# A hybrid attention block: constants merged so that matmul operands begin at multiples of 1024 bytes, and a background stream of weight sums paused in four gate blocks

## The chip, the cores and the metric

The kernel runs on one core of a Trainium2 chip. Its time is the device time of one execution in microseconds (us), as the median of several runs. A profiled execution gives the trace; its span is the time from the first to the last instruction.

## What is computed

One layer on 256 rows of 2048 features, all in float32. Heads have 128 features.

```python
h = rms_norm(x, g_mix)
proj = h @ w_in          # fq fk fv f_logit | sq sk sv | mq | 3 x 2048 gates
o_fox = forgetting attention, 6 heads, of normed fq, fk and of fv
o_sb  = stick-breaking attention, 6 heads, of sq, sk, sv
o_mem = attention of normed mq on 256 memory rows, 4 heads (rms_norm(mem) @ w_mem_kv)
g = sigmoid(gates + b_gate)
merged = g[0] * (o_fox @ w_br_fox) + g[1] * (o_sb @ w_br_sb) + g[2] * (o_mem @ w_br_mem)
x = x + merged @ w_out
h2 = rms_norm(x, g_ffn)
u = causal_depthwise_conv(h2 @ w_up)          # 2 x 5632 columns, 3 taps
u_gate, u_val = split(u)
out = x + (silu(u_gate) * u_val) @ w_down
```

## The kernel before, in words

**Split operands.** Every float32 matrix product is made of products of a 4-byte type that TensorE streams faster (`F32R`). Each weight piece is loaded as `raw` (128 partitions by 1024 elements) by a DMA that SyncE (SP) issues; ScalarE casts it to a high half `hi`, VectorE subtracts to get a low half `lo`. A product then takes three matmuls of 512 columns, activations high by weights high, low by high, high by low (lines 152 to 154, 286 to 288). In the up stage (lines 1146 to 1157) weights are the stationary operand: one matmul of 512 columns takes `hi` against both halves of the activations `hT`, one of 256 columns takes `lo` against the high half.

**Stages, in TensorE's order.** Memory keys and values; then products with `w_in` (`mq`, `f0` to `f4`, `s0` to `s4`) with the attention heads worked in between; the gates; the branch products (`b0` to `b3`); `w_out` (`o`); the up stage, 22 passes of four column tiles each (`u`, 11 groups of gate columns and 11 of value columns, each pass 16 steps of four pairs of matmuls); `w_down` (`d`). TensorE's instructions stand in program order in the gates, the branch products and most other stages.

**Blocks by seven.** Some pairs of k rows are multiplied with seven block products instead of eight (`seven`, `seven_here`, an "s" in a plan string; "e" is a pair by eight). They need sums of weight blocks (`T1` to `T4`) and of activation blocks (`FS1` to `FS4`). In the gates, `g_plans` gives four blocks with three such pairs each: `02`, `10`, `11`, `12`. Their weight sums are made on the spot: `prepared` issues two loads and four VectorE additions of 512 columns a pair.

**The stream of weight sums.** For `w_out` and `w_down` the weight sums are made ahead, in the background, by the generator `weight_sums` (lines 243 to 274). One round handles one half of a pair: two loads into a staging tile `pre`, then three VectorE additions (lines 267 to 269, of 512, 256 and 256 columns), then a store of the result to device memory (`kept`). There are 58 such halves, 14 for `w_out` and 44 for `w_down`. A later block by seven reads the `kept` sums in place of weights. The generator advances by one at each `tick()`: `period` is the number of ticks of a round, `add` the ticks between loads and additions, `store` those between loads and store, `slower` is added to the period once the attention heads are done ("heads" in `issued`). `tick` also advances the foreground generators (attention heads, transposes, gathers), and with `beside=False` only these. The first stream runs from the first projections to the end of the branch products ("merged"); what is left is made by two streams in the up stage (line 1088), with staging tiles of their own, a period of 8 and starts of 14 and 16 ticks.

**Order of the engines.** VectorE, ScalarE and SP work through their instructions in order. A scheduler places the instructions that are not pinned by `in_order`, so a changed tick changes the order on VectorE and SP around it.

**Addresses.** Tiles stand behind each other in SBUF in the order in which their pools and names come: `cst` (identity, `xres`, constants, `rbc`), then `wp` (`raw`, `hi`, `lo`), then `xt_pool` (`xT`, `hT`), `sm`, and the pools of the stage. A small tile takes a multiple of 32 bytes per partition. Before the change `qscale` is made 104 elements wide although one is used. In the program as built, `raw` begins at byte 40448 of a partition and `hi`, `lo`, `xT`, `memT`/`oT`/`aT` and the 14 blocks at 512 plus a multiple of 1024; `xres` (17920) does so too.

Of the kernel before, what the change touches and what calls it, by code (L numbers as in the profile page):

```python
# [9 lines left out]
F32 = mybir.dt.float32  # L10
# [5 lines left out]
P = 128  # L16
S = 256
NT = S // P
# [3 lines left out]
N_FOX, N_SB, N_MEM = 6, 6, 4  # L22
# [19 lines left out]
def hybrid_block(  # L42
# [28 lines left out]
    cst = ctx.enter_context(tc.tile_pool(name="cst", bufs=1))  # L71
# [9 lines left out]
    def bank(name):  # L81
        return pp.tile([P, 512], F32, tag="bank", name=name)
# [14 lines left out]
    def later(gen):  # L97
        waiting.append(gen)
# [3 lines left out]
    def tick(beside=True):  # L102
        if beside:
            for g in background:
                next(g, None)
        while waiting and len(active) < WINDOW:
            active.append([waiting.popleft(), 0])
        for a in list(active):
            if a[1] > 0:
                a[1] -= 1  # L110
                continue
            try:
                a[1] = next(a[0]) or 0
            except StopIteration:
                active.remove(a)
# [208 lines left out]
    def blocked(name, w, nb, n0, plan, pair, sums, raw_tile, t4_tile, gathered, ready=None, form=None, apart=None):  # L324

        wv = by_k(w)
        X = [[bank(f"x{name}{nb}_{t}_{n}") for n in range(2)] for t in range(NT)]
        Y = []
        ns = plan.count("s")

        def a_of(p, j, t):
            v = pair(p, j)
            return v[:, t * P : (t + 1) * P], v[:, S + t * P : S + (t + 1) * P]

        def f_of(p, f):
            v = sums(p, f)
            return v[:, 0], v[:, 1]

        def load(k):
            raw = raw_tile(f"raw_{name}{nb}_{k}")  # L340
            nc.sync.dma_start(raw, wv[:, k, n0 : n0 + PIECE])
            return raw

        def eight(p, first, last):
            by_bank = last and apart is not None
            w = []
            for j in range(2):
                w.append(parts(load(2 * p + j), f"{name}{nb}_{2 * p + j}"))
                if not by_bank:
                    for t in range(NT):  # L350
                        for n in range(2):
                            three(X[t][n], *a_of(p, j, t), w[j][n], first and j == 0, last and j == 1)
                tick()
            if by_bank:
                for t in range(NT):
                    for n in range(2):
                        m = 256 if (t, n) == (1, 1) else 512
                        for j in range(2):
                            wj = [part[:, :m] for part in w[j][n]]
                            three(X[t][n][:, :m], *a_of(p, j, t), wj, last=j == 1)  # L360
                        if m < 512:
                            apart.append(bank("apart")[:, m:])
                            for j in range(2):
                                wj = [part[:, m:] for part in w[j][n]]
                                three(apart[0], *a_of(p, j, t), wj, j == 0, j == 1)

        def seven(p, first, last):
            kept = sums_of[name, nb, p]
            raw0 = raw_tile(f"raw_{name}{nb}_{2 * p}")
            nc.sync.dma_start(raw0[:, :512], wv[:, 2 * p, n0 : n0 + 512])  # L370
            nc.sync.dma_start(raw0[:, 512:], kept[:, T3])
            raw1 = load(2 * p + 1)
            raw2 = raw_tile(f"raw_t_{name}{nb}_{p}")
            nc.sync.dma_start(raw2.rearrange("p (n c) -> p n c", n=2), kept[:, 0:4:3])
            raw3 = t4_tile(f"raw_t4_{name}{nb}_{p}")
            nc.sync.dma_start(raw3, kept[:, T4])
            B00, T3w = parts(raw0, f"{name}{nb}_{2 * p}")
            three(Y[0], *a_of(p, 0, 0), B00, first, last)
            three(Y[3], *f_of(p, FS3), T3w, first, last)
            B10, B11 = parts(raw1, f"{name}{nb}_{2 * p + 1}")  # L380
            three(X[0][0], *a_of(p, 1, 0), B10)
            three(X[0][1], *f_of(p, FS4), B11)
            tick()
            T1w, T2w = parts(raw2, f"t_{name}{nb}_{p}")
            three(Y[2], *f_of(p, FS1), T1w, first, last)
            three(Y[1], *f_of(p, FS2), T2w, first, last)
            (T4w,) = parts(raw3, f"t4_{name}{nb}_{p}")
            three(X[1][0], *a_of(p, 1, 1), T4w)
            tick()

        def prepared(p):
            raw0, raw1 = load(2 * p), load(2 * p + 1)
            t13, t42 = (t4_tile(f"t{i}_{name}{nb}_{p}") for i in range(2))
            b0, b1, u, v = (w.rearrange("p (n c) -> p n c", n=2) for w in (raw0, raw1, t13, t42))
            nc.vector.tensor_tensor(u[:, 0], b0[:, 0], b0[:, 1], ALU.add)
            nc.vector.tensor_tensor(u[:, 1], b0[:, 1], b1[:, 1], ALU.add)
            nc.vector.tensor_tensor(v[:, 1], u[:, 0], b1[:, 1], ALU.add)
            nc.vector.tensor_tensor(v[:, 0], v[:, 1], b1[:, 0], ALU.add)
            return raw0, raw1, t13, t42

        def seven_here(p, first, last):
            raw0, raw1, t13, t42 = ahead.pop(p)
            (B00,) = parts(raw0[:, :512], f"{name}{nb}_{2 * p}")
            three(Y[0], *a_of(p, 0, 0), B00, first, last)
            B10, B11 = parts(raw1, f"{name}{nb}_{2 * p + 1}")
            three(X[0][0], *a_of(p, 1, 0), B10)
            three(X[0][1], *f_of(p, FS4), B11)
            tick()
            T1w, T3w = parts(t13, f"t_{name}{nb}_{2 * p}")
            three(Y[2], *f_of(p, FS1), T1w, first, last)  # L410
            three(Y[3], *f_of(p, FS3), T3w, first, last)
            T4w, T2w = parts(t42, f"t_{name}{nb}_{2 * p + 1}")
            three(X[1][0], *a_of(p, 1, 1), T4w)
            three(Y[1], *f_of(p, FS2), T2w, first, last)
            tick()

        by_seven = seven_here if name == "g" else seven
        ahead = {}
        s, e = 0, ns
        for i, c in enumerate(plan):  # L420
            if c == "s":
                if s == 0:
                    if ready:
                        ready()
                    Y += [bank(f"y{name}{nb}_{j}") for j in range(4)]
                by_seven(s, s == 0, s == ns - 1)
                s += 1
                if s == ns:
                    later(gathered(n0, Y))
            elif c == "f":  # L430
                form()
            else:
                eight(e, i == 0, i == len(plan) - 1)
                e += 1
            if name == "g" and plan[i + 1 : i + 2] == "s":
                ahead[s] = prepared(s)
        finish()
        return X
# [42 lines left out]
    nc.gpsimd.affine_select(  # L481
        after_r, ones, pattern=[[-1, P]], compare_op=ALU.is_gt, fill=0.0, base=0, channel_multiplier=1
    )
    qscale = cst.tile([P, 104], F32, name="qscale")[:, :1]
    nc.vector.memset(qscale, SCALE)

    keep_busy(7)
# [61 lines left out]
        nc.vector.tensor_reduce(tot, ss, AX.X, ALU.add)  # L549
        rsqrt_mean(dst, tot, NT, D, name)  # L550

    rpair = cst.tile([P, 2, NT], F32, name="rpair")
    rstd, rneg = rpair[:, 0], rpair[:, 1]
    rstd_m = cst.tile([P, NT], F32, name="rstd_m")
    rstd_f = cst.tile([P, NT], F32, name="rstd_f")
    ssm = cst.tile([P, NT, 4], F32, name="ssm")
    ssx = cst.tile([P, NT, 4], F32, name="ssx")
    ssf = cst.tile([P, NT, 4], F32, name="ssf")
# [4 lines left out]
    gp = mix.enter_context(tc.tile_pool(name="gp", bufs=3))  # L563
# [108 lines left out]
    for k in range(KT):  # L672
# [18 lines left out]
        for _ in range(0 if k < 3 else 1 if k < 8 else 3):  # L691
            if squares:
                j, t = squares.popleft()
# [27 lines left out]
    def weighted(pT, v, h, oh, o):  # L721
# [7 lines left out]

    ps = proj(C_MQ, MEM_W, "mq")  # L730
    background.append(
        weight_sums(lambda name: gp.tile([P, 1024], F32, tag="pre", bufs=1, name=name), 5, 4, "merged", slower=3, add=2)
    )
    finish()
    qm = heads_of(block("qm"))
# [43 lines left out]
        nc.scalar.activation(vf[0][:, t], ps[t], AF.Copy, scale=rstd[:, t : t + 1])  # L779
    ps = proj(2048, 262, "f4")  # L780
    vf[1] = rows_of(block("vf1"))
    fl = cst.tile([P, NT, N_FOX], F32, name="fl")
    for t in range(NT):
        nc.scalar.activation(vf[1][:, t, :256], ps[t][:, :256], AF.Copy, scale=rstd[:, t : t + 1])
        nc.vector.scalar_tensor_tensor(
            fl[:, t], ps[t][:, 256:262], rstd[:, t : t + 1], bfor, ALU.mult, ALU.add
        )

    lf = cst.tile([P, NT, N_FOX], F32, name="lf")
    ab = cst.tile([P, NT, N_FOX], F32, name="ab")  # L790
    cq = cst.tile([P, NT, N_FOX], F32, name="cq")
    nc.scalar.activation(ab, fl, AF.Abs)
    nc.scalar.activation(ab, ab, AF.Exp, scale=-1.0)
    nc.scalar.activation(ab, ab, AF.Ln, bias=1.0)
# [160 lines left out]
    for m in range(2):  # L955
        gate = []
        for b, plan in enumerate(g_plans[m]):
            g, bias = [], []
# [26 lines left out]
            def ready():  # L985
                finish()
                if "heads" not in issued:
                    issued.add("heads")
                    later(sigmoids(gate[0] + gate[1]))
                biases()  # L990
# [23 lines left out]
        for n in range(2):  # L1014
            acc = gate[branches[0][3]][n]
            for i, (w, k0, nk, b) in enumerate(branches):
# [5 lines left out]
                for t in range(NT):  # L1022
                    g = gate[b][n]
# [227 lines left out]
```

## Time and profile before

| What | us |
|---|---|
| median of three runs | 1480.76 (1480.16 to 1483.44) |
| the profiled execution: its time | 1481.42 |
| the profiled execution: its span | 1479.7 |
| busy in the span: TensorE matmuls | 1470.7 (99%) |
| VectorE | 1192.9 (81%) |
| ScalarE | 839.5 (57%) |
| DMA queue of SP, share of 16 engines | 78.0% |

The granted TensorE clock was full throughout. A row of a group or of the timeline names the line, the engine, the operation, the tiles as out<-in, shapes and count. PE is TensorE, PEld its weight loads, DVE VectorE, ACT ScalarE, POOL GpSimd, SPq the DMA queue of SP. A matmul's duration (0.39 us for 512 columns) is longer than the distance to the next one's start, since matmuls overlap; distances of starts are what counts for the time. In brackets stands how long the engine was idle before, and who ended it.

### The profile page before, as it was taken

The page shows a single profiled execution, that of the slowest core. Times are in us where ns is not written, and L with a number is a line of the kernel's source. Part 1 is how long each engine was busy: PE and PEld are TensorE (multiplying, and loading weights), DVE is VectorE, ACT ScalarE, POOL GpSimd, SP SyncE. Part 2 cuts the span into 40 slices and gives each one's busy share as a digit, 9 for nine tenths or more (in the row PEclk, how much of TensorE's full clock was granted, in tenths as well). Part 3 has the DMA queues.
Part 4 walks back from the last instruction along what each step waited for, and adds up shares of the span by engine and source line. Part 5 has one row for each costly group of instructions (what it writes and reads, how often), then busy time and mean ns, then how long its engine had stood idle before and what let it go on. Part 6 is the DMA issues. An engine that isn't in the chain of part 4 may idle for free.

```text
span 1479.7 us, 20666 instructions
## 1 busy us (share of the span) xinstructions
PE 1470.7 (99%) x7337; PEld 1238.4 (84%) x7337; DVE 1192.9 (81%) x1818; ACT 839.5 (57%) x1194; POOL 18.6 (1%) x46
## 2 busy tenths in 40 slices
PE   9999999999999999999999999999999999999998
PEld 7888888888888878888888888888888888888887
DVE  5777676777688899988888889888777677997877
ACT  6755454455364455545666556556556565674664
POOL 0000000011000000000000000000000000000000
PEclk9999999999999999999999999999999999999999
DMA  9687797677877687978768889888766666798896
GB/s 306 202 274 222 219 297 229 206 248 252 282 238 251 215 273 254 299 239 289 256 204 274 275 277 292 264 279 282 212 186 177 195 182 202 237 318 270 260 328 224
DMA packets 205526, 369.42 MB, mean 250 GB/s; under 512 B 13530, under 2 KB 82030, under 8 KB 205166
## 3 DMA queue, kind: packets, MB, share of 16 engines
q1 hardware_dynamic: 204094, 365.99, 78.0%
q10 hardware_dynamic: 1328, 2.11, 0.4%
q8 instruction: 57, 0.93, 0.3%
q14 instruction: 47, 0.39, 0.1%
HBM read 335.54 MB, written 32.51 MB: 249 GB/s over the span
## 4 chain that ended last, share of the span: by engine, by line
PE 90%; DVE 5%; DMA 3%; issue 1%; ACT 1%; POOL 0%; SPq 0%; DVEq 0%; ACTq 0%; POOLq 0%
PE u L1154 22%; PE u L1155 11%; PE xd L287 4%; PE xd L286 4%; PE xd L288 4%; PE f L288 2%; PE f L286 2%; PE f L287 2%; PE s L286 2%; PE s L288 2%; PE s L287 2%; PE xg L288 2%; PE g L286 2%; PE g L288 2%; PE g L287 2%; PE xg L286 2%
## 5 line engine op out<-in xcount | busy, mean ns | idle before, releaser
L1154 PE MATMUL u<-hT,hi_u 128*128 128x512 f32 x1232 | 436.2, 399 | 0.0
L1155 PE MATMUL u<-hT,lo_u 128*128 128x256 f32 x1232 | 345.9, 281 | 0.0
L142 DVE TENSOR_TENSOR lo_u<-raw_u,hi_u 128x1024 fp32r<-128x1024 f32 x176 | 215.4, 1224 | 86.4 <-ACT hi_u L141 84.8
L1154 PEld LDWEIGHTS u<-hT,hi_u 128*128 128x128 f32 x1232 | 231.5, 188 | 57.5
L141 ACT CAST hi_u<-raw_u 128x1024 fp32r<-128x1024 f32 x176 | 184.7, 1050 | 147.7 <-PE u L1154 128.9
L1155 PEld LDWEIGHTS u<-hT,lo_u 128*128 128x128 f32 x1232 | 232.7, 189 | 0.0
L281 DVE TENSOR_TENSOR lo_d<-raw_d,hi_d 128x1024 fp32r<-128x1024 f32 x88 | 106.7, 1222 | 20.5 <-ACT hi_d L280 17.8
L280 ACT CAST hi_d<-raw_d 128x1024 fp32r<-128x1024 f32 x88 | 92.0, 1054 | 48.2 <-PE xd L287 22.2
L280 ACT CAST hi_g<-raw_g 128x1024 fp32r<-128x1024 f32 (+1 forms) x64 | 61.9, 972 | 39.2 <-DMA raw_g<-in_w_in_dram 16.1
L281 DVE TENSOR_TENSOR lo_g<-raw_g,hi_g 128x1024 fp32r<-128x1024 f32 (+1 forms) x64 | 71.3, 1120 | 3.4 <-ACT hi_g L280 3.3
L141 ACT CAST hi_f<-raw_f 128x1024 fp32r<-128x1024 f32 (+1 forms) x40 | 38.6, 967 | 51.2 <-PE f L287 46.5
L286 PE MATMUL xd<-hi_d,aT 128*128 128x512 f32 x170 | 66.2, 389 | 0.0
L288 PE MATMUL xd<-lo_d,aT 128*128 128x512 f32 x170 | 66.2, 389 | 0.0
L287 PE MATMUL xd<-hi_d,aT 128*128 128x512 f32 x170 | 66.1, 389 | 0.0
L142 DVE TENSOR_TENSOR lo_f<-raw_f,hi_f 128x1024 fp32r<-128x1024 f32 (+1 forms) x40 | 44.7, 1119 | 25.7 <-ACT hi_f L141 23.1
L141 ACT CAST hi_s<-raw_s 128x1024 fp32r<-128x1024 f32 (+1 forms) x40 | 38.4, 960 | 45.0 <-PE s L287 25.5
L1154 PE MATMUL u<-hT_rest,hi_u 128*128 128x512 f32 x176 | 63.1, 398 | 0.0
L142 DVE TENSOR_TENSOR lo_s<-raw_s,hi_s 128x1024 fp32r<-128x1024 f32 (+1 forms) x40 | 44.7, 1118 | 22.7 <-ACT hi_s L141 22.1
L141 ACT CAST hi_b<-raw_b 128x1024 fp32r<-128x1024 f32 x32 | 33.7, 1052 | 50.9 <-DMA raw_b<-in_w_br_sb_dram 16.0
L1126 ACT ACTIVATE y<-u,taps 128x256 f32<-128x256 f32 x88 | 49.3, 595 | 13.2 <-DVE u L1123 13.2
L142 DVE TENSOR_TENSOR lo_g<-raw_g,hi_g 128x1024 fp32r<-128x1024 f32 x32 | 39.2, 1229 | 21.1 <-ACT hi_g L141 20.8
L288 PE MATMUL xg<-lo_g,xT 128*128 128x512 f32 x140 | 54.8, 392 | 1.2 <-DVE lo_g L281 1.2
(481 smaller groups left out, 3509.5 us busy)
## 6 DMA issues: line engine op xcount, KB each, us to landing
raw_u<-in_w_up_dram SPq DMA_DIRECT2D x176, 512.0 KB, 4.7
raw_g<-in_w_in_dram SPq DMA_DIRECT2D x96, 512.0 KB, 4.7
raw_d<-in_w_down_dram SPq DMA_DIRECT2D x66, 512.0 KB, 5.1
pre_d<-in_w_down_dram SPq DMA_DIRECT2D x88, 256.0 KB, 4.3
kept_d<-pre_d SPq DMA_DIRECT2D x44, 512.0 KB, 5.3
raw_f<-in_w_in_dram SPq DMA_DIRECT2D x32, 512.0 KB, 5.0
raw_s<-in_w_in_dram SPq DMA_DIRECT2D x32, 512.0 KB, 5.0
raw_o<-in_w_out_dram SPq DMA_DIRECT2D x25, 512.0 KB, 6.3
```

The lines of the kernel that those rows point to most:

```text
L141: pin(nc.scalar.copy(hi[:, :m], raw[:, :m]))
L142: pin(nc.vector.tensor_tensor(lo[:, :m], raw[:, :m], hi[:, :m].bitcast(F32), ALU.subtract))
L280: nc.scalar.copy(hi[:, :n], src)
L281: nc.vector.tensor_tensor(lo[:, :n], src, hi[:, :n].bitcast(F32), ALU.subtract)
L286: fix(nc.tensor.matmul(o, lhsT=ah, rhs=w[0], start=first, stop=False))
L287: fix(nc.tensor.matmul(o, lhsT=al, rhs=w[0], start=False, stop=False))
L288: fix(nc.tensor.matmul(o, lhsT=ah, rhs=w[1], start=False, stop=last))
L1126: nc.scalar.activation(y, u[:, 2:], AF.Identity, scale=tap(2), bias=tap(3))
L1154: nc.tensor.matmul(ps[i], lhsT=hi[:, j, c], rhs=hT(k + j), start=first, stop=False)
L1155: nc.tensor.matmul(ps[i][:, :S], lhsT=lo[:, j, c], rhs=hT(k + j)[:, :S], start=False, stop=last)
```

## The change

Three edits.

1. In blocks called with the name "g", that is the four gate blocks with pairs by seven, ticks advance the foreground alone: `tick()` in `eight`, `seven` and `seven_here` becomes `go_on()`, which is `tick(beside=name != "g")`. The stream stands still there and goes on in the branch products.
2. The first stream's period goes from 5 to 6 ticks, and `slower` from 3 to 2. What it has not done by "merged" is done by the two streams of the up stage, whose own numbers are unchanged.
3. `rpair`, `rstd_m` and `rstd_f` become one tile `scales`, `fl`, `lf`, `ab` and `cq` one tile `logits`, and `qscale` loses its unused columns. The tiles behind them begin 512 bytes earlier: `raw` at byte 39936, and `hi`, `lo`, `xT`, `memT`/`oT`/`aT` and the blocks at multiples of 1024. `xres` stays where it is.

```diff
+        go_on = lambda: tick(beside=name != "g")
+
         def eight(p, first, last):
...
                             three(X[t][n], *a_of(p, j, t), w[j][n], first and j == 0, last and j == 1)
-                tick()
+                go_on()
...
         def seven_here(p, first, last):
...
             three(X[0][1], *f_of(p, FS4), B11)
-            tick()
+            go_on()
...
             three(Y[1], *f_of(p, FS2), T2w, first, last)
-            tick()
+            go_on()
...
-    qscale = cst.tile([P, 104], F32, name="qscale")[:, :1]
+    qscale = cst.tile([P, 1], F32, name="qscale")
...
-    rpair = cst.tile([P, 2, NT], F32, name="rpair")
-    rstd, rneg = rpair[:, 0], rpair[:, 1]
-    rstd_m = cst.tile([P, NT], F32, name="rstd_m")
-    rstd_f = cst.tile([P, NT], F32, name="rstd_f")
+    scales = cst.tile([P, 4, NT], F32, name="scales")
+    rstd, rneg, rstd_m, rstd_f = (scales[:, i] for i in range(4))
...
-        weight_sums(lambda name: gp.tile([P, 1024], F32, tag="pre", bufs=1, name=name), 5, 4, "merged", slower=3, add=2)
+        weight_sums(lambda name: gp.tile([P, 1024], F32, tag="pre", bufs=1, name=name), 6, 4, "merged", slower=2, add=2)
...
-    fl = cst.tile([P, NT, N_FOX], F32, name="fl")
+    logits = cst.tile([P, 4, NT * N_FOX], F32, name="logits").rearrange("p i (t h) -> p i t h", t=NT)
+    fl, lf, ab, cq = (logits[:, i] for i in range(4))
...
-    lf = cst.tile([P, NT, N_FOX], F32, name="lf")
-    ab = cst.tile([P, NT, N_FOX], F32, name="ab")
-    cq = cst.tile([P, NT, N_FOX], F32, name="cq")
```

The programs as built hold the same instructions on every engine, and TensorE, ScalarE and GpSimd run them in the same order but for six places on ScalarE where neighbours change. On VectorE and SP the additions, loads and stores of the stream stand later. Before, 35 halves are done before `w_out`'s stage and 23 in the up stage (its passes for columns 0 to 27); after the change it is 23 and 35 (columns 0 to 39). In the blocks `02`, `10`, `11` and `12` none stands after the change, where eight stood before.

More of the change, by code (lines that the diff above doesn't have):

```diff
@@ L407, in seven_here @@
             three(X[0][1], *f_of(p, FS4), B11)
-            tick()
+            go_on()
             T1w, T3w = parts(t13, f"t_{name}{nb}_{2 * p}")
@@ L414, in seven_here @@
             three(Y[1], *f_of(p, FS2), T2w, first, last)
-            tick()
+            go_on()
         by_seven = seven_here if name == "g" else seven
```

## The prediction

> **What bounds the kernel now.** I read the page first: span, engine shares, chain of waits.
>
> ```profile
> span 1479.7 us, 20666 instructions
> PE 1470.7 (99%) x7337; PEld 1238.4 (84%) x7337; DVE 1192.9 (81%) x1818; ACT 839.5 (57%) x1194; POOL 18.6 (1%) x46
> PE 90%; DVE 5%; DMA 3%; issue 1%; ACT 1%; POOL 0%; SPq 0%; DVEq 0%; ACTq 0%; POOLq 0%
> ```
>
> TensorE sets the end. The change leaves its instruction list and order as they are (7272 entries in both built programs, equal but for a tile's name), so time can come from two places alone: stalls of TensorE, and the spacing at which its matmuls follow each other. I take them in turn.
>
> Stalls first, by stage. The second view is the table of busy time by stretch: three of the four gates' blocks made by seven products (`g_plans`; 493.5 to 621.3), the up stage while the stream of weight sums runs, and the up stage after it has ended. Columns: stretch, length, then busy time (instructions) of TensorE, weight loads, VectorE, ScalarE and GpSimd, clock, DMA share, GB/s.
>
> ```profile
> 493.50:536.20 42.70, 42.70 (x193) 35.05 (x193) 40.33 (x54) 22.90 (x26) 0.00 (x0) 1.00 0.79 248
> 536.20:579.30 43.10, 42.07 (x185) 34.18 (x184) 42.27 (x55) 24.07 (x26) 0.00 (x0) 1.00 0.83 265
> 579.30:621.30 42.00, 41.81 (x185) 34.31 (x184) 40.78 (x53) 23.61 (x25) 0.00 (x0) 1.00 0.84 268
> 776.30:1070.40 294.10, 294.10 (x1668) 255.14 (x1667) 249.54 (x431) 172.14 (x261) 0.00 (x0) 1.00 0.86 270
> 1070.40:1251.30 180.90, 180.90 (x1027) 156.88 (x1026) 135.06 (x225) 104.78 (x160) 0.00 (x0) 1.00 0.64 186
> ```
>
> In the blocks by seven VectorE is as good as full: 40.33 of 42.70 us, 42.27 of 43.10, 40.78 of 42.00. In the up stage it is 85% busy with the stream (249.54 of 294.10) and 75% without (135.06 of 180.90), and the clock is 1.00 everywhere. The third view is TensorE's timeline at the five places where a low half (`lo_b`, `lo_g`) comes latest from VectorE: the first right behind a block by seven, three inside such blocks, the last at the end of the branch products.
>
> ```profile
> 450.36 0.39 PE L287 MATMUL b<-hi_b,oT 128*128 128x512 f32 x1
> ...
> 451.04 0.39 PE L287 MATMUL b<-hi_b,oT 128*128 128x512 f32 x1
> 452.10 0.50 PE L288 MATMUL b<-lo_b,oT 128*128 128x512 f32 x1 [0.67 <-DVE lo_b L142]
> ...
> 539.13 0.39 PE L287 MATMUL xg<-hi_g,xT 128*128 128x512 f32 x1
> 540.10 0.50 PE L288 MATMUL xg<-lo_g,xT 128*128 128x512 f32 x1 [0.58 <-DVE lo_g L281]
> 540.43 0.40 PE L286 MATMUL xg<-hi_g,xT 128*128 128x512 f32 x1
> ...
> 543.40 0.39 PE L287 MATMUL xg<-hi_g,xT 128*128 128x512 f32 x1
> 544.24 0.50 PE L288 MATMUL xg<-lo_g,xT 128*128 128x512 f32 x1 [0.45 <-DVE lo_g L281]
> ...
> 585.64 0.39 PE L287 MATMUL xg<-hi_g,xT 128*128 128x512 f32 x1
> 586.21 0.50 PE L288 MATMUL xg<-lo_g,xT 128*128 128x512 f32 x1 [0.19 <-DVE lo_g L281]
> ...
> 663.34 0.39 PE L287 MATMUL b<-hi_b,oT 128*128 128x512 f32 x1
> 664.31 0.50 PE L288 MATMUL b<-lo_b,oT 128*128 128x512 f32 x1 [0.58 <-DVE lo_b L142]
> ```
>
> Undisturbed, 512 columns follow each other at 0.227 us (450.36 to 451.04 is three steps). A stall costs the distance of the two starts less 0.227, and 0.10 more at the next step (540.10 to 540.43 is 0.33). So: 451.04 to 452.10 costs 0.93, 539.13 to 540.10 costs 0.84, 543.40 to 544.24 costs 0.71, 585.64 to 586.21 costs 0.44, 663.34 to 664.31 costs 0.84. The first four, which the pause can reach, are 2.92 us.
>
> **The change: the pause.** By the order of the changed program 12 half-pairs of sums leave the part before `w_out`'s stage and go into the up stage (35 halves were done before, now 23), and none is added in the gates' blocks by seven. Each is three VectorE additions, two loads and one store. Their price there, and what queues behind them at the worst place:
>
> ```profile
> L267 DVE TENSOR_TENSOR pre_d<-pre_d x44: 682/685/693, 286.7 to 1037.4; 128x512 f32<-128x512 f32 x44
> 532.99 0.69 DVE L267 TENSOR_TENSOR pre_d<-pre_d 128x512 f32<-128x512 f32 x1
> 533.59 0.75 DVE L970 SCALAR_TENSOR_TENSOR g<-gw,rpair,bg 128x512 f32<-128x512 f32 x1
> 534.25 0.42 DVE L268 TENSOR_TENSOR pre_d<-pre_d 128x256 f32<-128x256 f32 x1
> 534.59 0.68 DVE L982 TENSOR_TENSOR gw<-gw,yg 128x512 f32<-128x512 f32 x1
> 535.19 0.42 DVE L269 TENSOR_TENSOR pre_d<-pre_d 128x256 f32<-128x256 f32 x1
> 535.52 0.75 DVE L970 SCALAR_TENSOR_TENSOR g<-gw,rpair,bg 128x512 f32<-128x512 f32 x1
> 536.19 2.72 DVE L994 SCALAR_TENSOR_TENSOR g<-xg,rpair,g 128x512 f32<-128x512 f32 x4
> 538.82 1.22 DVE L281 TENSOR_TENSOR lo_g<-raw_g,hi_g 128x1024 fp32r<-128x1024 f32 x1
> ...
> 542.97 1.22 DVE L281 TENSOR_TENSOR lo_g<-raw_g,hi_g 128x1024 fp32r<-128x1024 f32 x1
> ```
>
> By the distances of the starts a half takes 0.60 (532.99 to 533.59) + 0.34 + 0.33 = 1.27 us of the queue. VectorE has no idle time from there to 542.97, and the four evacuations at 536.19 have their banks by then (the last `X` is finished as the block ends at 536.20, the first earlier), so all behind moves up by 1.27. In the changed order `lo_g` of the first stall even stands ahead of the evacuations. That stall goes whole: −0.84. TensorE then asks for the second `lo_g` 0.84 earlier and gets it 1.27 earlier: of the delay (544.24 − 543.40 − 0.23 = 0.61) 0.43 goes and some 0.18, with its 0.10, stays: −0.43. At 585.64 VectorE is 1.27 us ahead by the same step, more than the 0.44: all goes. For the first place the rows are these:
>
> ```profile
> 445.00 0.69 DVE L267 TENSOR_TENSOR pre_d<-pre_d 128x512 f32<-128x512 f32 x1
> ...
> 447.20 0.42 DVE L269 TENSOR_TENSOR pre_d<-pre_d 128x256 f32<-128x256 f32 x1
> ...
> 450.83 2.35 DVE L142 TENSOR_TENSOR lo_b<-raw_b,hi_b 128x1024 fp32r<-128x1024 f32 x2
> ```
>
> A half stands there too, in a queue without idle time up to the late `lo_b`, and in the changed order it is gone: −0.93. Together −2.64.
>
> What pays for it: at the end of the branch products the third addition of a half (0.34) now stands between the products that `lo_b` of 664.31 waits behind, where none stood, and I charge +0.34. Above nothing because VectorE is late there already; at worst all three land behind the wait, +1.27, at best they fall into VectorE's idle time, 0. Before the heads the period of the stream is 6 ticks instead of 5, after them 6 + 2 = 5 + 3; no late sum is on TensorE's path there, so 0, with ±0.5 for the attention chains whose additions change places (the nearest rows: stalls of 0.44 to 0.93). The sums of `w_out` are still stored before its stage begins, those of `w_down` by the up stage's column group 36 of 0 to 40, a stage ahead of their use: no wait of SP on a store that comes later.
>
> **The change: more of the stream in the up stage.** Passes at 1070 to 1251 get what those at 776 to 1070 had. Thirteen passes in 294.10 us are 22.62 each, eight in 180.90 are 22.61: the stream costs TensorE nothing there, though VectorE goes from 75% to 85% and DMA from 0.64 to 0.86. The cover is TensorE itself; were it gone, a half would cost 1.27 us, 12 of them 15.2. I take 0.
>
> **The change: addresses.** Merging small tiles moves every operand tile behind `rbc` by 512 bytes: `raw`, `hi`, `lo`, `xT`/`hT` and the rest begin at odd multiples of 512 before and at multiples of 1024 after. The small merged tiles themselves are used by the same instructions. What bounds the price is the second kind of time, spacing. The view is TensorE's timeline in the up stage, first and last row of two runs of matmul pairs (512 columns of `hi`, 256 of `lo`), and the grouped rows of the second run:
>
> ```profile
> 759.87 0.40 PE L1154 MATMUL u<-hT,hi_u 128*128 128x512 f32 x1
> ...
> 775.82 0.40 PE L1154 MATMUL u<-hT_rest,hi_u 128*128 128x512 f32 x1
> 776.74 0.40 PE L1154 MATMUL u<-hT,hi_u 128*128 128x512 f32 x1
> ...
> 844.22 0.40 PE L1154 MATMUL u<-hT,hi_u 128*128 128x512 f32 x1
> ```
> ```profile
> L1154 PE MATMUL u<-hT,hi_u 128*128 128x512 f32 x167 | 59.1, 399 | 0.0
> L1154 PE MATMUL u<-hT_rest,hi_u 128*128 128x512 f32 x24 | 8.6, 399 | 0.0
> ```
>
> The second run has 167 + 24 = 191 steps in 67.48 us, 353.3 ns each. The first is the last 47 pairs of the first pass, 46 steps in 15.95 us: 346.7 ns. The same code on the same tiles, then, has two rates, and it changed from the one to the other behind a few transposes (`hT`, `rp`) that stand inside these passes. From 776.3 to 1251.3 all 1344 pairs go at the slow rate; at the fast one they would take 1344 × 6.6 ns = 8.9 us less. Bounds of the edit: −8.9, and a mirror of it, +8.9. Both rates occur at the old addresses, and weights at even and odd multiples of 512 alternate inside every step without a difference, so nothing in this trace ties the rate to an address. The order of matmuls and transposes ahead of the run is unchanged, so I expect the same rate: 0.
>
> The Trainium skill, page "SBUF — State Buffer", the section on the DMA port swizzle, gives SBUF lines of 16 bytes, and its section on who interferes with whom says that TensorE waits on no one. Odd multiples of 512 are then as good as multiples of 1024, and the sum would be the one below without the case of the fast rate; the trace agrees as far as the alternating weights go, and has no moving operand at a multiple of 1024 to show the rest.
>
> **Sum.** −2.64 + 0.34 = −2.3; the other block by seven and the start of `w_out`'s stage lose sums from the queue as well, for which I allow −0.2, an estimate under the smallest stall priced above (0.44): −2.5. The profiled execution took 1481.4 us, its span 1479.7; that becomes 1478.9 and 1477.2. The runs' median, 1480.76, lies 0.66 below, so the forecast is **1478.2**.
>
> **Rivals.**
> 1. *The up stage runs at the fast rate.* The new addresses, or another phase at the restart after `rp`, let all passes go at 346.7 ns as the first one does. For it: the rate exists, and addresses are the only thing that changes there. Against it: two rates at the old addresses, weights that show no difference, and an unchanged order. 1478.2 − 8.9 = 1469.3.
> 2. *The matmuls' rhythm gets worse.* One mechanism with a place and a price: the up stage's pairs fall into a third, slower rhythm at the new addresses, or the stretches at 0.227 us lose theirs. From 0.003 us a pair on (1344 × 0.003 = 4.0) it eats more than the pause brings; at the mirror price of 6.6 ns it is 1478.2 + 8.9 = 1487.1. For it: two rhythms seen, so a third is not far-fetched. Against it: the stages of 512 columns alone keep 0.227 everywhere in this trace.
> 3. *The stalls only move.* VectorE stays 90% busy in the blocks by seven, and `prepared`'s four additions with the block's low halves are enough to be late; the pause then brings nothing: 1480.8. For it: the second stall at 544.24 lies behind `prepared`, not behind a sum of the stream. Against it: the queue is unbroken, and 1.27 us less is 1.27 us less.
>
> **How the numbers follow.** Chances: forecast 0.45, rival 1 0.34, rival 2 0.12, rival 3 0.09. A measurement of this kernel can tell about 0.2% from no change, 3.0 us, so from 1477.8 down it is faster. The forecast's own range is 1476.0 to 1480.0, by +1.27 − 0.34 at the branch products, ±0.5 for the attention chains and 0.3 for the second stall; it lies on that line, and I give 0.19 of its 0.45 to faster and 0.26 to same. Faster 0.34 + 0.19 = 0.53, same 0.26 + 0.09 = 0.35, slower 0.12. The range must reach rival 1, 1469.3 with the forecast's own slack: 1467.5 to 1480.9; outside lie rival 2 and tails, under 0.2.
>
> **What would show it.** VectorE's busy time in the blocks by seven falls by 2 to 3 us each. The waits at 452.10, 540.10 and 586.21 are gone, the one at 544.24 is under 0.3, the one at 664.31 is not smaller. The passes of column groups 28 to 36 in the up stage have VectorE at 85% and still the length of the others. The length of a pass decides the rest: 22.6 us says forecast, 22.2 rival 1, 23 rival 2. I am wrong if the blocks by seven keep their length, or if any stage away from these places changes by more than 1 us.

## The result and the profile after

The changed kernel takes 1476.08 us (median of six runs, 1475.54 to 1476.35); the kernel before took 1481.16 us beside it (six runs, 1480.16 to 1487.36). The ratio is 0.9958 with a 95% interval of 0.9941 to 0.9975: 0.4% faster. The forecast was 1478.2 in a range of 1467.5 to 1480.9.

The page of the changed kernel, its span, its engines and its chain of waits:

```profile
span 1474.3 us, 20665 instructions
PE 1468.7 (100%) x7337; PEld 1239.0 (84%) x7337; DVE 1195.8 (81%) x1818; ACT 840.3 (57%) x1194; POOL 20.4 (1%) x46
PE 98%; DMA 0%; DVE 0%; ACT 0%; SPq 0%; POOL 0%; issue 0%; POOLq 0%; DVEq 0%
```

VectorE and DMA held 8% of the chain before and nothing now. TensorE's busy time fell by 2.0 us (in part because a matmul that came late was counted 0.50 us instead of 0.39) and its idle time by 3.4; together that is the 5.4 us by which the span fell. The waits of TensorE that the list still has in this execution are at the start and in the attention part (it leaves out waits of 0.15 us and less):

```profile
PE spare L91 <- DVE qscale L487: 1.2, 1, 1.2
PE kv L153 <- DVE memT L184: 0.4, 1, 0.4
PE r L895 <- DVE ls L891: 0.2, 1, 0.2
```

Not one row with `lo_b` or `lo_g` is left. The table of busy time by stretch, for the same three blocks by seven, and for the part of the up stage that the stream has newly reached (columns as before):

```profile
491.30:533.70 42.40, 42.40 (x193) 35.19 (x192) 36.70 (x44) 22.79 (x26) 0.00 (x0) 1.00 0.64 194
533.70:575.50 41.80, 41.80 (x185) 34.30 (x184) 38.65 (x47) 23.93 (x26) 0.00 (x0) 1.00 0.70 214
575.50:617.20 41.70, 41.70 (x185) 34.25 (x184) 38.87 (x47) 24.30 (x26) 0.00 (x0) 1.00 0.70 220
...
1064.90:1178.00 113.10, 113.10 (x643) 98.14 (x642) 97.58 (x172) 65.81 (x100) 0.00 (x0) 1.00 0.86 273
```

VectorE's busy time (the third of the engines) fell by 3.6, 3.6 and 1.9 us in the three blocks, in 10, 8 and 6 instructions; 2 to 3 us in each were forecast. In the new part of the up stage it is at 86% (97.58 of 113.10), and five passes still take 113.10 us, 22.62 each.

Where the 5.4 us came from, by the distances from a stage's first matmul to the next stage's first, in the two profiled executions:

| Stretch | before | after | difference | forecast |
|---|---|---|---|---|
| `s1` (attention beside it) | 26.33 | 25.87 | −0.46 | 0 ± 0.5 for this row and the next |
| `s4` | 15.82 | 15.29 | −0.53 | |
| the rest up to block `02` (all in the first 15 us) | | | −0.3 | 0 |
| first products behind block `02` | 9.13 | 8.16 | −0.97 | −0.93 |
| block `10` | 42.63 | 42.37 | −0.26 | −0.2 for this row and `w_out` |
| block `11` | 43.11 | 41.77 | −1.34 | −0.84 − 0.43 |
| block `12` | 41.97 | 41.72 | −0.25 | −0.44 |
| first products behind block `12` | 8.25 | 8.16 | −0.09 | 0 |
| end of the branch products | 9.03 | 8.16 | −0.87 | +0.34 |
| first half of `w_out` | 42.15 | 41.77 | −0.38 | with block `10` |
| each pass of the up stage from the third on | 22.61 | 22.61 | 0 | 0 |

Below, a stall is what a stretch takes beyond its shortest length in any run: 25.86 us for `s1`, 8.16 for each of the three short stretches, 41.48 for blocks `11` and `12`, 41.77 for the first half of `w_out`.

### The profile page after: what moved, and what is told of

It reads as the page before. It is cut to its first block, busy times and chain, and to the rows that moved or that the text cites. A ratio compares the mean times of both kernels' runs of the same rounds, so it can differ in the third digit from the quotient of the medians.

```text
span 1474.3 us, 20665 instructions
## 1 busy us (share of the span) xinstructions
PE 1468.7 (100%) x7337; PEld 1239.0 (84%) x7337; DVE 1195.8 (81%) x1818; ACT 840.3 (57%) x1194; POOL 20.4 (1%) x46
## 4 chain that ended last, share of the span: by engine, by line
PE 98%; DMA 0%; DVE 0%; ACT 0%; SPq 0%; POOL 0%; issue 0%; POOLq 0%; DVEq 0%
PE u L1152 22%; PE u L1153 11%; PE xd L288 4%; PE xd L287 4%; PE xd L286 4%; PE xg L288 3%; PE xg L287 3%; PE xg L286 3%; PE f L288 2%; PE f L286 2%; PE f L287 2%; PE s L286 2%; PE s L288 2%; PE s L287 2%; PE g L286 2%; PE g L288 2%
## 5 line engine op out<-in xcount | busy, mean ns | idle before, releaser
L141 ACT CAST hi_g<-raw_g 128x1024 fp32r<-128x1024 f32 x32 | 33.6, 1051 | 37.4 <-PE g L287 35.1
```

What stands on the lines that cost most here:

```text
L141: pin(nc.scalar.copy(hi[:, :m], raw[:, :m]))
```

## The experiments

### The parts alone: addresses, stream, pause, period

`e1_addresses` is the kernel before with the third edit alone (`scales`, `logits`, narrow `qscale`).

```diff
-    qscale = cst.tile([P, 104], F32, name="qscale")[:, :1]
+    qscale = cst.tile([P, 1], F32, name="qscale")
...
+    scales = cst.tile([P, 4, NT], F32, name="scales")
...
+    logits = cst.tile([P, 4, NT * N_FOX], F32, name="logits").rearrange("p i (t h) -> p i t h", t=NT)
```

> The kernel before with the merged constants alone: operands at multiples of 1024 bytes, the stream as it was. My theory, that addresses change nothing: span 1479 to 1481 us, up-stage passes of 22.6 us, the five waits for a low half (at about 451, 539, 543, 586 and 663 us) still there at 0.4 to 0.9 us each. Rival, that the addresses bring part of the gain: span 1475 to 1478 us, and the waits or the spacing of matmuls smaller.

Measured: 1481.06 us, ratio 0.9989 (0.9975 to 1.0004), span 1480.1. The five stalls that were looked for are where they were, in other sizes: 0.77 behind block `02`, 1.23 and 0.49 in `11` and `12`, 0.71 at the end of the branch products. The others changed more, at the same stream: 0.49 behind block `12` (0.09 before), 2.15 in the first half of `w_out` (0.38), 0.15 in `s1` (0.46). TensorE's waits for low halves in its profile:

```profile
PE b L288 <- DVE lo_b L142: 1.0, 3, 0.4
PE xg L288 <- DVE lo_g L281: 0.8, 3, 0.4
PE yo L288 <- DVE lo_t_o L281: 0.5, 1, 0.5
PE yo L288 <- DVE lo_o L281: 0.5, 1, 0.5
```

Every pass of the up stage has its length of before. The addresses do nothing that these runs can tell from none.

`e2_stream` is the changed kernel with the old constants: the first two edits alone.

```diff
+        go_on = lambda: tick(beside=name != "g")
...
-        weight_sums(lambda name: gp.tile([P, 1024], F32, tag="pre", bufs=1, name=name), 5, 4, "merged", slower=3, add=2)
+        weight_sums(lambda name: gp.tile([P, 1024], F32, tag="pre", bufs=1, name=name), 6, 4, "merged", slower=2, add=2)
```

> The changed kernel with the old constants: pause and new period, operands at odd multiples of 512 bytes. My theory: the whole gain is here, span 1474 to 1475.5 us, no wait for a low half left. Rival, that addresses count: span 1476.5 us or more.

Measured: 1475.66 us, ratio 0.9952 (0.994 to 0.9965), span 1473.8, no wait for a `lo_b` or `lo_g`. The whole gain is the stream's.

`e3_pause` has the first edit alone (`go_on`; the period stays 5 and 3).

> The kernel before with the pause in the blocks by seven alone, period 5 and 3 more after the heads as before. My theory: the waits in and behind the blocks by seven go, and with them about 2.6 to 4 us: span 1475.5 to 1477.5 us. The stalls of the attention chains before 310 us stay as they were. Rival, that the pace of the stream matters everywhere: less than half of the gain, span above 1477.5 us.

Measured: 1478.2 us, ratio 0.9972 (0.9961 to 0.9983), span 1477.7. The stalls in and behind the blocks by seven are gone, although one half is still added in `02` and one in `12`, 36.9 us into the block. Left are those at the end of the branch products (1.02) and in `w_out` (1.18), and the one in `s1` is larger, 1.38 us. The profiled execution, the slowest of six, lies 0.2 us above the span that the theory gave; the spans of the other five, 1475.6 to 1477.2, lie within it. Its waits:

```profile
PE fa L727 <- DVE fx L840: 1.1, 1, 1.1
PE b L288 <- DVE lo_b L142: 0.7, 1, 0.7
PE yo L288 <- DVE lo_o L281: 0.5, 1, 0.5
```

`e4_period` has the second edit alone: 6 and 2, and ticks in the blocks by seven as before.

> The kernel before with the period of 6 and 2 more after the heads alone, no pause. My theory: the queue of VectorE in the blocks by seven is as full as before, three or more waits for a low half of 0.4 us or more stay there; only up to 1 us is won, in the attention chains before 310 us: span 1478.5 to 1480.5 us. Rival, that the new phase of the stream does it and not the pause: span under 1477 us.

Measured: 1477.34 us, ratio 0.9968 (0.9955 to 0.9981), span 1475.4. My theory missed here, and the rival holds. I had looked for at least three of the stalls to stay, since the blocks by seven keep their sums; one row of waits for a low half was left, and behind 400 us only two stalls are larger than in the changed kernel, 0.41 behind block `12` and 0.70 in the second column of `b2`:

```profile
PE b L288 <- DVE lo_b L142: 0.4, 1, 0.4
```

Yet there are as many sums. The first additions of the halves in blocks `10`, `11` and `12`, by the view of their line, in the kernel before (493.5 to 621.3 us):

```profile
L267 DVE TENSOR_TENSOR pre_d<-pre_d x6: 684/686/687, 515.1 to 617.3; 128x512 f32<-128x512 f32 x6
```

and in `e4_period` (491.5 to 617.3):

```profile
L267 DVE TENSOR_TENSOR pre_d<-pre_d x6: 684/685/691, 501.5 to 605.0; 128x512 f32<-128x512 f32 x6
```

Six halves in both, and with the two in `02` eight. What differs is their place: the last one begins 4.0 us ahead of the end of block `12` before, and 12.3 us ahead of it here. In each of the four blocks the second half begins 38.0 to 39.4 us behind the block's first matmul before, and 29.2 to 30.1 us in `e4_period`. So at the same number of halves it is their place in the block that decides. No run asks how near to the end is too near. Pause and period bring 0.28% and 0.32% alone and 0.48% together. They take some of the same stalls away, so they can't add up in full, but the intervals are too wide to show that by the times.

### The stall at the end of the branch products

Here the forecast had the sign wrong. The timeline of the kernel before, SP's, ScalarE's and VectorE's rows for the `raw_b` behind the late `lo_b`:

```profile
650.43 0.88 SPq L258 DMA_DIRECT2D pre_d<-in_w_down_dram  x2
651.42 0.40 SPq L140 DMA_DIRECT2D raw_b<-in_w_br_sb_dram  x1
...
657.73 1.05 ACT L141 CAST hi_b<-raw_b 128x1024 fp32r<-128x1024 f32 x1 [4.13 <-DMA raw_b<-in_w_br_sb_dram]
658.68 0.58 ACT L175 CAST mT<-mt 128x512 fp32r<-128x512 f32 x1
...
659.29 0.69 DVE L176 TENSOR_TENSOR mT<-mt,mT 128x512 fp32r<-128x512 f32 x1 [2.74 <-ACT mT L175]
...
663.04 1.22 DVE L142 TENSOR_TENSOR lo_b<-raw_b,hi_b 128x1024 fp32r<-128x1024 f32 x1
```

and, from the view of waits on SP's queue from 640 to 660 us:

```profile
SPq L258 <- DMA kept_d<-pre_d: 3.1, 1, 3.1
```

Read from the top: the stream's loads into `pre_d` stood on SP for 3.1 us, until the store of the previous half out of the same tile had landed. The last weights of the branch products stood in line behind them. ScalarE sat 4.13 us for those weights, with the cast for `mT` queued behind; VectorE sat 2.74 us for that cast, and then had `lo_b` ready late. VectorE had been idle: it was not its load alone that made the stall. After the change the weights are issued early, and all three additions of a half stand in front of `lo_b`:

```profile
639.15 4.33 SPq L140 DMA_DIRECT2D raw_b<-in_w_br_sb_dram  x3
...
652.09 0.68 DVE L267 TENSOR_TENSOR pre_d<-pre_d 128x512 f32<-128x512 f32 x1
652.80 0.42 DVE L268 TENSOR_TENSOR pre_d<-pre_d 128x256 f32<-128x256 f32 x1
...
654.94 0.42 DVE L269 TENSOR_TENSOR pre_d<-pre_d 128x256 f32<-128x256 f32 x1
...
657.62 1.22 DVE L142 TENSOR_TENSOR lo_b<-raw_b,hi_b 128x1024 fp32r<-128x1024 f32 x1
659.17 0.39 PE L287 MATMUL b<-hi_b,oT 128*128 128x512 f32 x1
```

`lo_b` begins 1.55 us ahead of TensorE's last matmul before it (657.62 to 659.17), where it had 0.30 before (663.04 to 663.34). Two runs test the reading.

`e7_one_less` is the kernel before whose first stream ends one half earlier, so that this pair of loads isn't there.

```diff
-        while halves and end not in issued:
+        while halves and end not in issued and not (end and len(halves) == 24):
```

> The kernel before, but its first stream stops one half earlier (34 halves instead of 35): the load at about 650 us, which waits 3.1 us on SP for a store to land, is left to the up stage; all additions ahead of the wait at 664.31 us stay. Theory, that this wait comes from the queue of SP (the load of raw_b stands behind the waiting load, hi_b and the cast of mT behind it are late, VectorE idles 2.7 us): the wait of 0.84 us at about 664 us is gone, span about 1478.8 us. Rival, that VectorE's products there are simply too many: it stays at 0.7 us or more.

Measured in one run: 1479.2 us, span 1477.5. This stall is gone and so are those in `w_out`; those of the blocks by seven stay (0.73 behind `02`, 1.15 in `11`, 0.49 in `12`, 0.85 behind `12`). The proof is thinner than I wished: SP now stood 2.9 us at a load of kept sums that waits for the same store, and `raw_b` came only some 1.1 us earlier against TensorE.

`e10_loads_apart` is the kernel before with the first stream's loads issued by GpSimd, so that no load of `pre` can stand ahead of weights on SP.

```diff
-                    nc.sync.dma_start(
+                    (nc.gpsimd if end else nc.sync).dma_start(
```

> The kernel before with the loads of its first stream (two for each of 35 halves) issued by GpSimd instead of SP; stores stay on SP, and from the third block of the gates on VectorE's order is that of before. Theory (the stall of 0.84 us at the end of the branch products came from SP: a load of the stream waited there for a store to land, and the weights behind it were late): that stall is under 0.2, while the stalls in and behind the blocks by seven, which are VectorE's queue, stay, the first three at 0.4 us or more each: span 1478.4 to 1479.3, time some 1480. Rival A (all of these stalls are VectorE's load): the stall at the end of the branch products stays at 0.7 or more and the span is 1479.5 to 1480.5. Rival B (all of them come from SP's loads standing in line): those in the blocks by seven go too, span 1475 to 1476.5. GpSimd's own issue may cost something; a longer span with new waits on DMA tiles would say so and leave this open.

Measured: 1500.52 us, ratio 1.0131 (1.0103 to 1.0158), span 1499.3. The total is a miss, and none of the spans expected holds: the kernel lost 17.6 us up to block `02` and 3.1 in it, while VectorE stood at additions whose loads came late from GpSimd. Its wait for them, in the list of waits:

```profile
DVE pre_d L267 <- DMA pre_d<-in_w_down_dram: 35.3, 8, 8.0
```

Behind 500 us VectorE's order is that of before and the stages can be compared. Timeline of `e10_loads_apart` at the end of its branch products, GpSimd, SP, ScalarE, VectorE, TensorE:

```profile
670.32 1.44 POOL L258 DMA_DIRECT2D pre_d<-in_w_down_dram  x2 [23.23 <-DMA kept_d<-pre_d]
670.71 0.37 SPq L140 DMA_DIRECT2D raw_b<-in_w_br_sb_dram  x1
...
675.53 1.05 ACT L141 CAST hi_b<-raw_b 128x1024 fp32r<-128x1024 f32 x1 [1.22 <-DMA raw_b<-in_w_br_sb_dram]
...
677.41 0.69 DVE L176 TENSOR_TENSOR mT<-mt,mT 128x512 fp32r<-128x512 f32 x1
...
681.14 1.23 DVE L142 TENSOR_TENSOR lo_b<-raw_b,hi_b 128x1024 fp32r<-128x1024 f32 x1
...
684.11 0.39 PE L287 MATMUL b<-hi_b,oT 128*128 128x512 f32 x1
```

It is now GpSimd's loads that the store releases (GpSimd had been idle for 23.23 us, not all of it for the store), the cast waits 1.22 us instead of 4.13, `mT` waits for nothing, and `lo_b` begins 2.97 us ahead instead of 0.30. The 2.67 us gained are nearly the 2.74 us for which VectorE had been idle. The stretch takes 8.16 us. The stall in `w_out` is gone as well, while the blocks by seven keep theirs: `11` and `12` take 43.13 and 42.00 us, where they took 43.11 and 41.97. The expectation said that a longer span with new waits would leave this open, and for the total it does; by these stretches alone two kinds of stall are told apart, as the theory has it: SP's line made the one at the end of the branch products, VectorE's queue those of the blocks by seven.

### The two rhythms of the up stage

The forecast's widest bound was not the stream but the 353.3 ns per pair of matmuls, against 346.7 ns in 47 pairs of the first pass. Four runs ask what chooses between them.

`e5_grouped` is the changed kernel with the four matmuls of 512 columns of a k step first and the four of 256 columns behind them.

```diff
                         nc.tensor.matmul(ps[i], lhsT=hi[:, j, c], rhs=hT(k + j), start=first, stop=False)
+                    for i in range(4):
+                        c = slice(i * P, (i + 1) * P)
                         nc.tensor.matmul(
                             ps[i][:, :S], lhsT=lo[:, j, c], rhs=hT(k + j)[:, :S], start=False, stop=last
```

> The changed kernel with the up stage's matmuls in another order: in each k step first the four of 512 columns, then the four of 256, the same matmuls and weights. Theory, that the slow rate of 353 ns a pair is a rhythm which the alternation of 512 and 256 columns locks into, while runs of one length keep their 227 and 120 ns: a pass takes 22.2 us in place of 22.6, span about 1474.3 - 9 = 1465.3 us. Rival, that the slow rate belongs to the stage (its VectorE and ScalarE work, its reads of SBUF): passes stay at 22.6 us, span 1474 us. A share of the transitions between lengths may keep a cost: 22.3 us.

Measured: 1472.67 us, ratio 0.9944 (0.993 to 0.9958), span 1471.7. From the third pass on each takes 22.45 us, 350.8 ns per pair: between the two rhythms. Grouping recovers some 3.2 us, where some 9 were expected. (The stall at the end of the branch products is back in this profile with 0.92 us, at a stream unchanged from the changed kernel's. The weights were issued at 640.18 us instead of 639.15, and VectorE has no idle time from 648.96 us to `lo_b` at 658.56, with all three additions of a half on the way. So that place has a thin margin after the change too, and by these rows the additions count there; no run takes them out.)

`e6_restarts` is the changed kernel with n spare transposes ahead of a pass, one ahead of the third, two ahead of the fourth, and so on up to 20. They are added work: only the pass's own rhythm counts.

```diff
+            for _ in range(max(0, f0 // 2 + s - 1)):
+                nc.tensor.transpose(ps[0][:, :P], ident, ident)
```

> The changed kernel with a block of dummy transposes of the identity ahead of passes 3 to 22 of the up stage, one in pass 3, two in pass 4 and so on to 20 (their results are overwritten by the pass). Theory, that the rate of a pass is set by the phase in which the matmuls restart behind transposes: passes take one of two rates, 346.7 or 353.3 ns a pair, by the number of transposes ahead of them, some fast and some slow. Rival, that the first pass was fast because its VectorE and ScalarE had no convolution to do: all of them stay at 353 ns.

Measured in one run: 1492.56 us. Behind each restart the rhythm is one of the two, to the end of the pass: the fast one behind 1, 3, 6, 8 to 12, 14 and 16 to 20 transposes, the slow one behind 2, 4, 5, 7, 13 and 15. The first transposes of three passes one after the other:

```profile
1046.11 1.47 PE L1146 MATMUL u<-ident 128*128 128x128 f32 x12
...
1069.60 1.58 PE L1146 MATMUL u<-ident 128*128 128x128 f32 x13
...
1093.65 1.69 PE L1146 MATMUL u<-ident 128*128 128x128 f32 x14
```

The pass with 12 takes 23.49 us (1046.11 to 1069.60), that with 13 takes 24.05 (to 1093.65). One transpose is 0.11 (1.58 − 1.47); the other 0.45 are 64 pairs at about 7 ns, the slow rhythm.

`e8_one_restart` is the changed kernel with a single transpose ahead of the third pass:

```diff
+            if (f0, s) == (4, 0):
+                nc.tensor.transpose(ps[0][:, :P], ident, ident)
```

> The changed kernel with one transpose (128x128, into the first bank that the pass then overwrites) ahead of the third pass of the up stage, and nowhere else. Theory (the rhythm is chosen by the phase at which the pairs of 512 and 256 columns start again after something else, and then holds for as long as pairs alone follow): the 20 passes from there on take 22.19 us instead of 22.61, 20 x 0.42 = 8.4 us less; the transpose and its restart cost 0.2; span 1474.3 - 8.2 = 1466.1, time about 1467.8. Rival A (the rhythm drifts back to the slow one, as it did in the second pass of before): the third pass takes 22.2, later ones 22.61; span 1474.1. Rival B (what is slow is another thing, the stream or the pieces that arrive): all passes 22.61, span 1474.5.

Measured: **1467.05 us** (1466.9 to 1467.55), ratio 0.9898 (0.9882 to 0.9914), span 1465.3. All passes behind it take 22.19 us. The grouped rows of the up stage from the third pass to its end, in the changed kernel (793.7 to 1245.8 us):

```profile
L1152 PE MATMUL u<-hT,hi_u 128*128 128x512 f32 x1120 | 396.6, 399 | 0.0
...
L1152 PE MATMUL u<-hT_rest,hi_u 128*128 128x512 f32 x160 | 57.4, 399 | 0.0
```

and in `e8_one_restart` (793.7 to 1236.9):

```profile
L1154 PE MATMUL u<-hT,hi_u 128*128 128x512 f32 x1119 | 388.8, 394 | 0.0
...
L1154 PE MATMUL u<-hT_rest,hi_u 128*128 128x512 f32 x160 | 56.4, 394 | 0.0
```

1280 pairs in 452.1 us are 353.2 ns each; 1279 in 443.2 us are 346.5. A single transpose, 0.1 us of work, saves some 8.4 us (20 passes at 0.42), and what it sets holds to the end of the stage. It beats both kernels.

`e9_old_addresses` puts the same transpose into the kernel before.

> The kernel before, addresses and stream as they were, with the same single transpose ahead of the third pass of the up stage. Theory (addresses have no part in the rhythm): passes from the third on 22.19 us as in the changed kernel with that transpose, span 1479.7 - 8.2 = 1471.5 give or take 1.5 for the stalls of before. Rival (operands at multiples of 1024 bytes are what lets the fast rhythm hold): passes stay at 22.61 or fall back to it, span 1479.5 or more.

Measured in one run: 1472.38 us, span 1470.6; passes of 22.19 us from the fourth on. Its row for the same stretch (799.0 to 1242.2 us):

```profile
L1156 PE MATMUL u<-hT,hi_u 128*128 128x512 f32 x1119 | 388.8, 394 | 0.0
```

The same numbers as at the new addresses, so which of the two sets of addresses is used has no part in it.

## Why the prediction came out as it did

**TensorE sets the end, and stalls are what the stream can give.** Right. `e1_addresses` and `e2_stream` part the change cleanly: all of the gain lies in stalls of TensorE, but for 0.3 us in the first 15 us of the profiled execution.

**The stalls of the blocks by seven.** Right, and well sized: 0.93 forecast against 0.97 behind block `02`, 1.27 against 1.34 in `11`, 0.44 against 0.25 in `12`; with 0.26 in `10` and 0.09 behind `12` it is 2.9 us. In `12` that is little more than half of what was forecast. `e3_pause` shows that the pause alone takes them away. It is not needed for that: in `e4_period` a shifted phase takes away most of them with all eight halves left in the blocks, so 1.27 us of additions in a block cost time by where they stand, and not by themselves. The −0.2 for block `10` and `w_out` came out at −0.64; the stall in `w_out` went in `e7_one_less` and `e10_loads_apart` too, without the pause.

**The end of the branch products.** The step that failed: "the third addition of a half (0.34) now stands between the products that `lo_b` of 664.31 waits behind", charged at +0.34, "above nothing because VectorE is late there already". It came out at −0.87, and that is 1.21 of the 2.9 us by which the span fell further than forecast (5.4 against 2.5). VectorE was late because it had sat idle for 2.74 us in front of `mT`, where the rows that the prediction shows don't reach. Behind that idle time stood ScalarE, behind ScalarE the weights, and behind them SP, held for 3.1 us by a load that waited for a store. The prediction did look for such a wait, but only at stores of `w_out`'s and `w_down`'s sums that come after their readers, not at the staging tile's own store ahead of its next load. `e10_loads_apart` shows the chain by taking its first link away; `e5_grouped` shows that a cost of the kind that was charged can still come, 0.92 us in an execution whose weights were issued 1.03 us later.

**The attention chains, 0 ± 0.5.** Their reason failed: "no late sum is on TensorE's path there". One is. In the timeline of the kernel before, VectorE in `s1` (and TensorE's row that waits):

```profile
223.37 0.69 DVE L267 TENSOR_TENSOR pre_o<-pre_o 128x512 f32<-128x512 f32 x1 [1.28 <-DMA pre_o<-in_w_out_dram]
224.10 0.42 DVE L268 TENSOR_TENSOR pre_o<-pre_o 128x256 f32<-128x256 f32 x1
224.56 0.42 DVE L269 TENSOR_TENSOR pre_o<-pre_o 128x256 f32<-128x256 f32 x1
...
226.38 0.55 DVE L838 COPY fx<-fb 128x384 f32<-128x384 f32 x1
226.98 0.70 PE L725 MATMUL fa<-fx,vf 128*128 128x256 f32 x2 [0.20 <-DVE fx L838]
```

and after the change, where no half stands at that place:

```profile
223.68 1.22 DVE L142 TENSOR_TENSOR lo_s<-raw_s,hi_s 128x1024 fp32r<-128x1024 f32 x1 [1.86 <-ACT hi_s L141]
...
225.16 0.55 DVE L836 COPY fx<-fb 128x384 f32<-128x384 f32 x1
...
226.34 0.59 PE L725 MATMUL fa<-fx,vf 128*128 128x256 f32 x2
```

An addition waits for its own load, and all of VectorE's queue with it, `fx` among it, for which TensorE's attention product waits. How much that costs is a matter of the execution. With the same order in `s1`, VectorE waited for this load 0.17 us in `e7_one_less`, 0.95 in `e1_addresses`, 1.28 in the kernel before, 1.37 in `e9_old_addresses` and 2.18 in `e3_pause`, and the stall was 0, 0.15, 0.46, 0.55 and 1.38 us. In all runs with the new period it is 0.

`s4` gained 0.53 for the same edit: it takes 15.82 or 15.83 us in every kernel run here with a period of 5 and 15.29 or 15.30 in every one with 6. The wait there is that of TensorE's product `r` for `ls`, which is cast from `sb` once GpSimd has masked it. GpSimd's and VectorE's rows in the kernel before:

```profile
306.35 2.37 POOL L868 TENSOR_SCALAR_AFFINE_SELECT sb<-sb 128x128 f32<-128x128 f32 x2 [1.76 <-DVE sb L886]
306.11 2.46 DVE L142 TENSOR_TENSOR lo_g<-raw_g,hi_g 128x1024 fp32r<-128x1024 f32 x2
```

and after the change:

```profile
305.61 1.85 POOL L866 TENSOR_SCALAR_AFFINE_SELECT sb<-sb 128x128 f32<-128x128 f32 x2 [1.76 <-DVE sb L884]
306.52 0.78 DVE L267 TENSOR_TENSOR pre_o<-pre_o 128x512 f32<-128x512 f32 x1
```

GpSimd's row holds two masks. The second ends 0.15 or 0.16 us behind the end of the VectorE instruction beside it (308.72 against 308.57, 307.46 against 307.30). With the period of 6 that instruction is an addition of the stream (0.78 us) and no longer a second low half (1.31), and the masks end 0.52 us sooner. The second mask takes 1.27 us in all six profiles with the old period and 0.74 in all six with the new one; no run tests this alone. Here an addition of the stream saves time. Together `s1` and `s4` are −0.99, outside the ±0.5.

**The up stage, 0 for 12 more halves.** Right: 22.62 us a pass with VectorE at 86%.

**The addresses, 0 with bounds of ∓8.9.** Right, and now shown: 0.9989 (0.9975 to 1.0004) alone, and passes of 22.19 us at both sets of addresses. The Trainium skill, page "SBUF — State Buffer", the section on the DMA port swizzle, with its lines of 16 bytes, spoke for that; with matmul operands at multiples of 1024 as in `e1_addresses`, the trace agrees.

**The rivals.** The fast rate exists and can be had for all passes, as the first rival said; by the phase of a restart, not by addresses, and the change leaves that phase as it was. A worse rhythm did not come. That the stalls only move is refuted by the list of waits. The forecast was nearly even between faster and same for its own case; the result falls to the faster side by the two missed terms, and both happened to miss the same way. There is luck in the range too: 1476.08 lies just inside the 1476.0 to 1480.0 that the prediction gives for its own case, but the terms that it names for this reach down only to 1477.1 (1478.2 − 0.34 − 0.5 − 0.3). The stated range reached lower for the sake of the first rival, which did not come.

## What to carry to other kernels

The background stream of this kernel cost through its queues more than through its work: an addition that waited for its load, or a load that waited for the store out of its staging tile, held up everything behind it on its engine. When a low half or an evacuation is late, go back through each idle time ahead of it, engine by engine, until one is found that waits for nothing, before its queue is called full. And where thousands of equal matmuls set the time, compare their spacing between stretches; 7 ns a pair was worth more here than the whole edit.

## What the runs showed of the hardware that was not expected

Alternating matmuls of 512 and 256 columns, each with its own weights, have at least two stable rhythms, 353.3 and 346.7 ns a pair; whichever a restart falls into is held over 20 passes, some 450 us. All eight profiles with the original order of matmuls and no added transpose have the slow one from the second pass on. What the restart's phase must be is open: neither the parity nor the order of the transposes' number sorts the cases of `e6_restarts`.

The stalls of the kernel before are not of fixed size. With its stream and order, the one at the end of the branch products was 0.87 us in its own profile, 0.71 in `e1_addresses` and 1.60 in `e9_old_addresses`, and its six runs spread over 7.2 us; the changed kernel's six spread over 0.8. One of 18 executions of the kernel before beside `e1_addresses` took 1474.79 us, and one of that run's eleven 1473.57, some 7 us below the medians of their fellows. Neither was profiled, so it is open whether the fast rhythm came by itself there.
